# A hybrid mLSTM and sparse-attention block: head operands one head ahead, product buffers dealt anew, branch products with the mLSTM half first

## The chip, the cores and the metric

The kernel runs on one core of a Trainium2 chip. The metric is the device time of one execution in microseconds (us). A profile of one execution, with a row for each instruction and each transfer, shows where that time lies. Engines are called as in the profile: PE (TensorE's matmuls), DVE (VectorE), ACT (ScalarE), POOL (GpSimd), SP (SyncE, which only issues transfers here).

## The reference

T = 1024 tokens, D = 1024. One RMS norm, one wide projection, two mixers, gates, an output projection, and a feed-forward net:

```python
u = rms_norm(h, g_norm_mix); proj = u @ w_in + b_in
mq, mk, mv, mo, mi, mf, nq, nkv, ngate, merge = split_columns(proj, IN_SIZES)
y_m = mlstm_mixer(mq, mk, mv, mo, mi, mf, ...)       # 4 heads x 128, chunks of 128
y_n = nsa_mixer(nq, nkv, ngate, pe_cmp, w_cmp1, w_cmp2, rel_bias)   # 8 heads x 64
branch = einsum('btnw,nwd->btnd', stack([y_m, y_n]), w_branch)
h = h + sum(sigmoid(merge) * branch) @ w_out
f = rms_norm(h, g_norm_ffn)
h = h + (silu(f @ w_gate) * (f @ w_up)) @ w_down; out = rms_norm(h, g_final)
```

The mLSTM head multiplies, for each chunk, a masked decay matrix M (an exponential of it) with q·k, adds the carried state C scaled by S = exp(log_inter − m), and multiplies C by a decay for the next chunk.

## The kernel before, in words

All matmuls are float32 made of three fp32r products (`mm3`, L284: high·high, low·high and high·low parts), so each operand is split once: the high part on ACT, the low part on DVE or Pool.

**Order of the work.** Two ways. The first stages are planned by `Plan` (L63 on): steps are added with hand-written costs, and `run` (L128) deals them to the engines' in-order queues by earliest start and rank; a step with two alternatives goes to the engine that starts it first; a step with `fill=True` is taken only when PE has nothing else. The later stages are written in program order, which is then each engine's queue order.

**First tiles.** For the eight token tiles in the order `XO`, `norm` (L500) makes the norm, `trans` (L513) the transposes into UTH/UTL (u, high and low), `p0` (L544) the NSA values and gate columns, `forms` (L598) the sums of u that the products need. Merge tile 0 (one of 16 tiles of the merge gates' pre-activation, `merge_steps` L659, `merge_half` L679: 24 matmuls a half, its eviction on ACT at L686, then a store) lies between them as fill; both halves are evicted into piece ("x3", 1).

**Products.** The projection's other columns are 12 pairs of 256 columns (`PAIRS` L689). Each is made with seven products in place of eight (`product` L827), from raw weights (`load_raw` L699, pieces dealt by `RAWS` L693), whose sums are split (`prep` L739, operand buffers dealt by `WRING` L694) and whose results are combined (`finish` L769). Within this run `gates` (L903) writes the decay tables M and S to DRAM (d_M, d_S), and `compress` (L998) makes the compressed keys and values: it loads a DRAM copy, adds position columns for 32 windows (L1017, DVE or Pool) and multiplies by w_cmp (L1022).

**mLSTM heads.** `head_load(h)` (L1101) loads v, k, q, M, S, o on SP's queue, S and M by a broadcast read; `core(h)` (L1112) transposes v (L1125), masks M on Pool (L1133; half of head 0's on DVE), copies the decays out of S (L1134), multiplies S by q, then works through 8 chunks (L1143 to L1165), norms and gates, and stores d_ym. Merge tiles 1 to 3 (`merge_B` L1216) are fill beside them. The d_u tiles, parts of u that had been put aside in DRAM, are read back ahead of that by Pool's queue, and VHL (the NSA values, 2 MB) too, wherever the plan finds its place free.

**Attention and merge tiles 4 to 13.** A scheduler of its own; `load_pair` (L1287) loads a pair's q, k and bias tables (QA, KH, KL, FB, FW), for pair 0 on Pool's queue.

**Branch stage.** Merge tiles 14 and 15 run while `load_y` (L1740) reads the y tiles: its step k issues tile k's loads (one of 512 KB for the four mLSTM tiles, two for the four NSA tiles) into a ring of six and splits tile k − 2 into YH and YL (NSA tiles: a sum on DVE first, L1753). A merge tile yields 16 times (`fm_tile` L1248: eight k steps a half, 24 matmuls) and after its fifth k step of the first half it splits the weight of the next job (`split` L243: ACT at L256, then Pool in quarters at L262 or DVE at L264). Then come the branch products d = 0 to 7: for each token half, b = 0 (mLSTM, YH tiles 0 to 3) and b = 1 (NSA, 4 to 7), 12 matmuls each, times the sigmoid of the stored merge gate, added and split.

```python
for z, _ in enumerate(merge_tile(j, gring, psD, 8)):
    if z % 3 == 1:
        next(ly, None)
```

After that the output projection and the feed-forward net, a second plan that the change doesn't touch.

## Time and profile before

| | |
|---|---|
| three runs | 1581.93, 1582.65, 1582.60 us (median 1582.6) |
| profiled execution | 1581.21 us |
| its span in the profile | 1579.4 us (1.8 us lie outside) |
| PE busy in the span | 1543.7 us (98%) |
| DVE, ACT, POOL busy | 1161.1, 772.9, 294.5 us |
| mean granted clock of PE | 0.988 |

A row of the trace names the start, the duration, the engine, the line, the operation, output <- input; in brackets the idle time of the engine before it and what ended it. From 780 us on, the feed-forward net and what leads to it, the stretches show PE busy almost without a break.

### The profile page before, as it was taken

What the parts mean: (1) busy time and instruction counts of PE and PEld (TensorE: products, weight loads), DVE (VectorE), ACT (ScalarE), POOL (GpSimd) and SP (SyncE); (2) the same over time, 40 slices, a digit from 0 to 9 for tenths busy, and PEclk for the clock granted to TensorE, in tenths of its full rate; (3) what the DMA queues carried; (4) which work ended last, traced back from release to release, by engine and by line L of the source; (5) the groups of instructions that cost most, each with busy time, mean ns of one, the idle gap of its engine ahead of it and who ended that gap; (6) DMA issues with size and microseconds to landing.
All of it is one profiled execution on the core that took longest, in us unless ns stands there. A gap on an engine that the chain in (4) does not pass through costs nothing.

```text
span 1579.4 us, 22540 instructions
## 1 busy us (share of the span) xinstructions
PE 1543.7 (98%) x7810; PEld 1304.3 (83%) x7810; DVE 1161.1 (74%) x2390; ACT 772.9 (49%) x1654; POOL 294.5 (19%) x410
## 2 busy tenths in 40 slices
PE   8998999989899999999999999999999999999997
PEld 7887888888699988888788888888888888888886
DVE  5988677657698868884656677666666666988996
ACT  5533333355588868784444453333333333454443
POOL 4658755223111311002002000000000000000130
PEclk9999999999999999999999999999999999999999
DMA  6656674598523632216556324222222223750302
GB/s 180 204 144 199 206 247 134 144 296 164 151 57 103 106 103 71 85 47 219 163 160 227 107 81 133 94 80 80 81 88 86 81 80 115 272 192 22 107 0 107
DMA packets 169899, 205.84 MB, mean 130 GB/s; under 512 B 10265, under 2 KB 128311, under 8 KB 169530
## 3 DMA queue, kind: packets, MB, share of 16 engines
q1 hardware_dynamic: 156584, 179.43, 36.3%
q0 software_dynamic: 12912, 24.65, 6.6%
q8 instruction: 61, 1.00, 0.3%
q14 instruction: 52, 0.43, 0.1%
q10 hardware_dynamic: 290, 0.33, 0.1%
HBM read 149.75 MB, written 62.48 MB: 134 GB/s over the span
## 4 chain that ended last, share of the span: by engine, by line
PE 89%; DVE 4%; DMA 4%; ACT 2%; POOL 1%; issue 1%; SPq 0%; DVEq 0%; ACTq 0%; POOLq 0%
PE PS L286 15%; PE PS L287 15%; PE PS L285 15%; PE PSA L285 5%; PE PSA L287 5%; PE PSA L286 5%; PE T L1437 4%; PE d L285 2%; PE d L287 2%; PE d L286 2%; PE obank L1457 2%; PE obank L1459 2%; PE br L286 2%; PE br L287 2%; PE br L285 2%; DMA XB<-d_S 1%
## 5 line engine op out<-in xcount | busy, mean ns | idle before, releaser
L1840 DVE TENSOR_TENSOR sl<-PS,sl 128x512 f32<-128x512 f32 x182 | 123.5, 688 | 100.8 <-PE PS L287 100.3
L1446 DVE TENSOR_TENSOR TL<-T,TH 128x512 fp32r<-128x512 f32 (+1 forms) x184 | 103.3, 581 | 31.8 <-ACT TH L1442 30.7
L1840 POOL TENSOR_TENSOR acc<-acc 128x512 f32<-128x512 f32 x6 | 9.2, 1545 | 617.6 <-DVE acc L1840 617.5
L1840 DVE TENSOR_TENSOR sl<-sl,sl 128x512 f32<-128x512 f32 (+1 forms) x130 | 88.4, 687 | 21.9 <-DMA d_h<-sl 7.2
L1442 ACT ACTIVATE TH<-T 128x512 fp32r<-128x512 f32 (+1 forms) x184 | 90.3, 510 | 28.7 <-PE T L1437 26.0
L1843 ACT ACTIVATE sl<-sl 128x512 f32<-128x512 f32 (+1 forms) x77 | 48.6, 632 | 57.9 <-PE PS L286 34.4
L1457 PE MATMUL obank<-TH,VHL 128*128 128x256 f32 x264 | 75.4, 309 | 0.0
L285 PE MATMUL d<-UTH,whi 128*128 128x512 f32 x176 | 71.9, 409 | 1.0 <-ACT mg L1274 0.7
L287 PE MATMUL d<-UTH,wlo 128*128 128x512 f32 x176 | 69.1, 392 | 0.0
L286 PE MATMUL d<-UTL,whi 128*128 128x512 f32 x176 | 69.0, 392 | 0.0
L1459 PE MATMUL obank<-TL,VHL 128*128 128x256 f32 x264 | 68.1, 282 | 0.0
L285 PE MATMUL PSA<-UTH,wOwhi 128*128 128x512 f32 x156 | 65.0, 417 | 2.3 <-ACT wOwhi L444 2.2
L285 PE MATMUL PS<-q 128*128 128x512 f32 x172 | 66.9, 389 | 0.0
L286 PE MATMUL PS<-q 128*128 128x512 f32 x172 | 66.9, 389 | 0.0
L287 PE MATMUL PS<-q 128*128 128x512 f32 x172 | 66.9, 389 | 0.0
L287 PE MATMUL PSA<-UTH,wOwlo 128*128 128x512 f32 x164 | 64.9, 396 | 0.0
L1843 ACT ACTIVATE q<-sl 128x512 fp32r<-128x512 f32 x74 | 43.1, 623 | 42.3 <-PE PS L286 32.2
L262 POOL TENSOR_TENSOR wlo<-raw,whi 128x256 fp32r<-128x256 f32 x44 | 32.1, 761 | 169.6 <-ACT whi L256 129.0
L286 PE MATMUL PSA<-UTL,wOwhi 128*128 128x512 f32 x156 | 62.0, 397 | 0.0
L1843 ACT ACTIVATE wh<-sl 128x512 fp32r<-128x512 f32 x39 | 24.6, 631 | 58.2 <-PE PS L286 40.8
L285 PE MATMUL br<-YH,whi 128*128 128x512 f32 x128 | 50.5, 395 | 2.0 <-ACT YH L281 2.0
L286 PE MATMUL br<-YL,whi 128*128 128x512 f32 x128 | 50.7, 396 | 0.5 <-DVE YL L282 0.5
(1380 smaller groups left out, 5075.7 us busy)
## 6 DMA issues: line engine op xcount, KB each, us to landing
d_gu<-sl SPq DMA_DIRECT2D x44, 256.0 KB, 2.2
rA<-in_w_in SPq DMA_DIRECT2D x18, 512.0 KB, 4.7
q<-d_mg SPq DMA_DIRECT2D x32, 256.0 KB, 3.0
d_rep<-d_row POOLq DMA_DIRECT2D x8, 960.0 KB, 6.6
sl<-in_w_down SPq DMA_DIRECT2D x15, 512.0 KB, 3.6
sl<-d_gu SPq DMA_DIRECT2D x15, 512.0 KB, 4.9
ra<-in_w_gate SPq DMA_DIRECT2D x14, 512.0 KB, 3.8
ra<-in_w_up SPq DMA_DIRECT2D x13, 512.0 KB, 4.5
```

The source lines that it names most:

```text
L262: nc.gpsimd.tensor_tensor(lo[:, zs], v[:, zs], cast32(hi)[:, zs], ALU.subtract)
L285: nc.tensor.matmul(ps, ah, bh, start=first, stop=False)
L286: nc.tensor.matmul(ps, ah, bl, start=False, stop=False)
L287: nc.tensor.matmul(ps, al, bh, start=False, stop=last)
L1437: nc.tensor.transpose(pt[:, z, P * r:P * r + P], e, ident)
L1442: nc.scalar.activation(hl[0][:, 0:m], pt[:, 0:m], AF.Copy)
L1446: nc.vector.tensor_tensor(hl[1][:, 0:m], pt[:, 0:m], cast32(hl[0])[:, 0:m], ALU.subtract)
L1457: nc.tensor.matmul(po, vv, th[:, z, :], start=(st[1] == 0), stop=False)
L1459: nc.tensor.matmul(po, vv, tl[:, z, :], start=False, stop=(st[1] == st[2]))
L1840: return pl.step(alts, lambda e: ENG[e].tensor_tensor(out_(), x(), y(), alu), reads, writes, **kw)
L1843: return pl.step((("ACT", cost),), lambda e: nc.scalar.activation(out_(), x(), fn), reads, writes, **kw)
```

## The change

It has five parts. *First tiles*: the norms are made in pairs, one tile ahead, with a small Newton step of five DVE operations for two tiles; p0 adds its bias in one DVE operation, and Pool copies the gate columns out; merge tile 0's halves become ordinary steps of a raised rank, with a piece each (x3 and g21). *Products*: raw pieces and operand buffers are dealt out anew (the first six operands in turn from two buffers); the last pair makes q = 4 third and holds its finish until q = 7. *Compression*: the windows' costs change. *mLSTM heads*: the decays are read by one broadcast load from d_S (DEC); M, q, k, v, S, o get new places, S that of v after v's transposes (head 0 has one of its own); masks and S·q are made on Pool one head ahead; the key weighting may go to ACT; the d_u tiles are restored in the last pair; VHL is loaded ahead of the last head, into the places that head 2 had for k, v and o. *Branch stage*: `load_y` steps at z % 2; the products of d = 0 and 1 run all b = 0 first, then b = 1, with eight gate pieces. The tail of the branch loop for d ≥ 2, `values` (the transposes of v, moved out of `core`) and some lines of tile sizes are left out here.

```diff
@@ -37,6 +37,7 @@
+MA_ = (60, 60)
@@ -497,18 +498,33 @@
-        def norm(i):
-            x_, st = xb[i], stA[:, i, :]
-            s = sb_[i] = K(st)
-            stp("ACT", 1250.0, lambda: nc.scalar.activation(sqA, flat(x_.ap), AF.Square, accum_out=st[:, 0:1]), [x_], [s, sq_A])
-            stp("DVE", 160.0, lambda: nc.vector.tensor_scalar(st[:, 0:1], st[:, 0:1], 1.0 / D, EPS, ALU.mult, ALU.add), (), [s])
-            stp("ACT", 210.0, lambda: nc.scalar.activation(st[:, 1:2], st[:, 0:1], AF.Sqrt), tabs[-1:], [s])
-            stp("DVE", 800.0, lambda: rstd_b(st), (), [s])
...
+        def norm(*ii):
+            n = XO.index(ii[0])
+            st = stA[:, n:n + len(ii), :]
+            s = K(st)
+            hbs = []
+            for i in ii:
+                sb_[i] = s
+                stp("ACT", 1250.0, lambda i=i: nc.scalar.activation(sqA, flat(xb[i].ap), AF.Square, accum_out=stA[:, XO.index(i), 0:1]), [xb[i]], [s, sq_A])
+            stp("DVE", 160.0, lambda: nc.vector.tensor_scalar(st[:, :, 0:1], st[:, :, 0:1], 1.0 / D, EPS, ALU.mult, ALU.add), (), [s])
+            stp("ACT", 210.0, lambda: nc.scalar.activation(st[:, :, 1:2], st[:, :, 0:1], AF.Sqrt), tabs[-1:], [s])
...
+            def newton():
+                y, v, t = (st[:, :, n:n + 1] for n in (2, 0, 3))
+                nc.vector.reciprocal(y, st[:, :, 1:2])
+                nc.vector.tensor_tensor(t, y, y, ALU.mult)
+                nc.vector.tensor_tensor(t, t, v, ALU.mult)
+                nc.vector.tensor_scalar(t, t, -0.5, 1.5, ALU.mult, ALU.add)
+                nc.vector.tensor_tensor(y, y, t, ALU.mult)
+            stp("DVE", 950.0, newton, (), [s])
+            for i in ii:
...
+            return hbs
@@ -561,13 +577,12 @@
-            stp("DVE", 420.0, lambda: nc.vector.tensor_tensor(vt, n4(ps.ap[:, 0:256]), n4(BB[:, 0:256]), ALU.add), [ps] + b_BB, [vb])
-            stp("DVE", 180.0, lambda: nc.vector.tensor_tensor(GT[:, i, :], ps.ap[:, 256:288], BB[:, 256:288], ALU.add), [ps] + b_BB, [b_GT])
+            stp("DVE", 450.0, lambda: nc.vector.tensor_tensor(VT[:, i % 2], ps.ap[:, 0:288], BB, ALU.add), [ps] + b_BB, [vb])
+            stp("Pool", 300.0, lambda: nc.gpsimd.tensor_copy(GT[:, i, :], VT[:, i % 2, 256:288]), [vb], [b_GT])
@@ -638,7 +653,7 @@
@@ -650,10 +665,23 @@
+        HN = {}
...
+        def tile(i):
+            n = XO.index(i)
+            trans(i, HN[i])
+            if n + 3 < NT:
+                load_x(XO[n + 3])
+            if n % 2 == 0:
+                norms(n + 1)
+            p0(i)
...
+        def norms(n):
+            HN.update(zip(XO[n:n + 2], norm(*XO[n:n + 2])))
+        load_x(XO[3])
+        norms(1)
...
-            load_x(XO[XO.index(i) + 2])
-            trans(i, norm(i))
-            p0(i)
+            tile(i)
@@ -676,12 +704,12 @@
-        def merge_half(t, half, mt, o, reads):
+        def merge_half(t, half, mt, o, reads, fill=True):
...
-                    [hb, lb] + reads(n), [ps], fill=True)
+                    [hb, lb] + reads(n), [ps], fill=fill)
@@ -690,17 +718,17 @@
-        RAWS = ["r1 r2", "g20 g10", "r0 r1", "r2 g20", "g10 r0", "r1 r2", "g20 g10", "r0 r1", "r2 g20", "g10 r0", "r2 g20", "r1 r0"]
-        WRING = ("w1", "w3", "w0", "w2")
+        RAWS = ["r1 r2", "r0 g20", "g10 r1", "r2 r0", "g20 g10", "r1 r2", "r0 g20", "g10 r1", "r2 r0", "g20 g10", "r1 r2", "r0 g20"]
+        WRING = ("w0", "w2", "w1", "w3")
...
-        def load_raw(m, after=0.0):
+        def load_raw(m, khs=(0, 1)):
...
-            for kh in range(2):
+            for kh in khs:
@@ -737,7 +765,7 @@
-            nm = WRING[nop[0] % 4]
+            nm = WRING[(nop[0] - 6) % 4 if nop[0] > 5 else 2 + nop[0] % 2]
@@ -851,11 +879,14 @@
+                if (m, 4) in pb:
+                    finish(m, (1, 0), pb[m, 4], v[3])
...
-                finish(m, (1, 0), ps, v[3])
+                if 3 in v:
+                    finish(m, (1, 0), ps, v[3])
@@ -877,26 +908,25 @@
-            if n < 2:
-                load_x(XO[n + 6])
-            trans(i, norm(i))
-            p0(i)
+            tile(i)
...
-            merge_half(0, z, mA, ("x3", 1), lambda n, z=z: [x for i in range(4 * z, 4 * z + 4) for x in (ub[i][0::2] if n >= 4 else ub[i][1::2])])
+                load_raw(1, (0,))
+            pA.boost = -MA_[z]
+            merge_half(0, z, mA, ("x3 g21".split()[z], 1), lambda n, z=z: [x for i in range(4 * z, 4 * z + 4) for x in (ub[i][0::2] if n >= 4 else ub[i][1::2])], fill=False)
...
-        load_raw(1)
+        load_raw(1, (1,))
...
-        seq += [(NP - 1, q) for q in (1, 2, 6, 7, 4, 5, 3)]
-        for n in range(4):
+        seq += [(NP - 1, q) for q in (1, 2, 4, 6, 7, 5, 3)]
+        for n in range(2):
@@ -970,6 +1000,8 @@
+            sd = d_S[:, P - 1:P]
+            load("Pool", 16, [(DEC, bass.AP(tensor=sd.tensor, offset=sd.offset, ap=[[0, P], [P, 32]]))], [b_MS], [b_dec], cost=700.0)
@@ -1015,7 +1047,7 @@
-                pA.step((("DVE", 1150.0), ("Pool", 1700.0)), windows, [kb, b_c], [fb_])
+                pA.step((("DVE", 1700.0), ("Pool", 4000.0)), windows, [kb, b_c], [fb_])
@@ -1037,16 +1069,68 @@
+        ubr = []
...
+        def restore():
+            ubr.extend([x for i in range(NT) for n, x in enumerate(ub[i]) if not (i % 2 and n % 2 == 0)])
+            for j in range(4):
+                cs = slice(P * (2 * j + 1), P * (2 * j + 2))
+                b = K(True, prior=fsb[4, j])
+                load("Pool", 512, [((UTH, UTL)[z][:, 0:4, cs], d_u[j][z]) for z in range(2)], [dub[j]], [b], cost=1400.0)
+                ubr.append(b)
...
+        HB = {}
+        HS = [("v2", "v3", "g10", "v0", "g20", "v1"), ("b0", "b1", "b2", "b3", "b4", None), ("g21", "v2", "v3", "g11", "v1", None), ("r1", "g01", "g10", "r0", "g20", None)]
...
+        def head_load(h, keys):
+            for key in keys:
+                n = "qkvMoS".index(key)
+                b = HB[h, n] = slot(HS[h][n]) if HS[h][n] else HB[h, 2]
+                if key in "MS":
+                    r0 = (d_M if key == "M" else d_S)[h:h + 1, :]
+                    src = bass.AP(tensor=r0.tensor, offset=r0.offset, ap=[[0, P], [4 * P, NT], [1, P]])
+                    load("SP", 512, [(lambda b=b: v8c(b), src)], [b_MS], [b], cost=600.0)
+                else:
+                    load("SP", 512, [(lambda b=b: flat(b.ap), d_mx[key][h])], [dst[key, h]], [b], cost=600.0)
...
+        v8c = lambda b: b.ap.rearrange("p a (c t) -> p (a c) t", t=P)
...
+        def values(h):
...
+        def scale_q(h):
+            SB, q = HB[h, 5], HB[h, 0]
+            for z in range(4):
+                zs = slice(2 * z, 2 * z + 2)
+                stp("Pool", 900.0, lambda zs=zs: nc.gpsimd.tensor_tensor(v8c(SB)[:, zs], v8c(q)[:, zs], v8c(SB)[:, zs], ALU.mult), [q], [SB])
...
+        def mask(h):
+            MB = HB[h, 3]
+            for z in range(4):
+                zs = slice(2 * z, 2 * z + 2)
+                stp("Pool", 900.0, lambda zs=zs: nc.gpsimd.tensor_tensor(v8c(MB)[:, zs], causal[:, None, :].to_broadcast([P, 2, P]), v8c(MB)[:, zs], ALU.subtract), b_rows[8:9], [MB])
...
-        b_MS, b_gc = K(True), K(True)
+        b_MS, b_gc, b_dec = K(True), K(True), K(True, prior=small + [sb_[i] for i in range(NT)])
+        DEC = MSC[:, 876:908]
...
-            if n > 3:
+            if n > 1:
@@ -1057,23 +1141,20 @@
+            if (m, q) == (NP - 1, 4):
+                restore()
...
+            if (m, q) == (8, 3):
+                head_load(0, "MqkS")
+                mask(0)
+                scale_q(0)
...
@@ -1092,48 +1173,15 @@
-        ring("dec", [MSC[:, 578 + 8 * z:586 + 8 * z] for z in range(2)], small)
...
-            stp("Pool", 250.0, lambda: nc.gpsimd.memset(MV[:, :, MD:MD + 1], 1.0), (), [MVb])
-            dec, ss = take("dec"), take("ss")
-            for z in range(2):
-                pv = K()
...
-            for z in range(4):
-                zs = slice(2 * z, 2 * z + 2)
-                if h == 0 and z < 2:
-                    stp("DVE", 400.0, lambda zs=zs: nc.vector.tensor_tensor(v8(MB)[:, zs], causal[:, None, :].to_broadcast([P, 2, P]), v8(MB)[:, zs], ALU.subtract), b_rows[8:9], [MB])
-                else:
-                    stp("Pool", 900.0, lambda zs=zs: nc.gpsimd.tensor_tensor(v8(MB)[:, zs], causal[:, None, :].to_broadcast([P, 2, P]), v8(MB)[:, zs], ALU.subtract), b_rows[8:9], [MB])
-            stp("DVE", 150.0, lambda: nc.vector.tensor_copy(dec.ap, v8(SB)[:, :, 127]), [SB], [dec])
-            for z in range(2):
-                ew(ANY, lambda z=z: SB.ap[:, z, :], lambda z=z: q.ap[:, z, :], lambda z=z: SB.ap[:, z, :], ALU.mult, [q, dec], [SB])
+            ss = take("ss")
@@ -1146,7 +1194,13 @@
-                stp("DVE", 340.0, lambda: nc.vector.tensor_scalar(KW[c].ap, pa_.ap[:, 128:256], E_.ap[:, 127:128], None, ALU.mult), [pa_, E_], [KW[c]])
...
+                def kw(e):
+                    if e == "DVE":
+                        nc.vector.tensor_scalar(KW[c].ap, pa_.ap[:, 128:256], E_.ap[:, 127:128], None, ALU.mult)
+                    else:
+                        nc.scalar.activation(KW[c].ap, pa_.ap[:, 128:256], AF.Copy, scale=E_.ap[:, 127:128])
+                pA.step((("DVE", 340.0), ("ACT", 340.0)), kw, [pa_, E_], [KW[c]])
@@ -1161,7 +1215,7 @@
-                        stt(350.0, lambda: CN.ap, lambda: CN.ap, dec.ap[:, c:c + 1], lambda: o(pu), ALU.mult, ALU.add, [pu, dec], [CN])
+                        stt(350.0, lambda: CN.ap, lambda: CN.ap, DEC[:, 4 * c + h:4 * c + h + 1], lambda: o(pu), ALU.mult, ALU.add, [pu, b_dec], [CN])
@@ -1216,22 +1270,35 @@
-                merge_half(t, z, mB, (("g00", "g01")[t % 2], z), lambda n: ubr if n == 4 else [])
...
+                merge_half(t, z, mB, ("g00", z), lambda n: ubr if n == 4 else [])
...
+        head_load(0, "vo")
+        values(0)
+        head_load(1, "Mqkv")
+        mask(1)
...
-        head_load(0)
-        head_load(1)
+        values(1)
+        head_load(1, "So")
+        scale_q(1)
+        merge_B(2, ("r2", "w0", "w2"))
...
-        head_load(2)
+        head_load(2, "Mqkv")
+        mask(2)
+        values(2)
+        head_load(2, "So")
+        scale_q(2)
+        merge_B(3, ("r2", "w1", "w3"))
...
-        head_load(3)
-        for t_ in range(2, NMB):
-            merge_B(t_, ("r2", ("w0", "w1")[t_ % 2], ("w2", "w3")[t_ % 2]))
+        head_load(3, "Mqkv")
+        mask(3)
+        values(3)
+        head_load(3, "So")
+        scale_q(3)
...
-        core(3)
...
+        core(3)
@@ -1759,7 +1826,7 @@
-                if z % 3 == 1:
+                if z % 2 == 1:
@@ -1771,19 +1838,57 @@
-        load_gates(0, 0)
-        for d in range(8):
+        wide = Pieces([q1_tile(n, F32)[:, z, :] for n in (5, 3) for z in range(4)])
+        gring, narrow = wide, gring
+        W = {}
...
+        def branch(d, half, b):
+            hs = slice(512 * half, 512 * half + 512)
+            sg = sgs[d, half]
+            nc.scalar.activation(sg[b], sg[b], AF.Sigmoid)
+            wh, wl = W[d]
+            ps = psD.tile([P, 512], F32, name=f"br{d}{half}{b}", tag="D", bufs=8)
+            for k in range(4):
+                kk = 4 * b + k
+                mm3(ps, wh[:, kk, :], wl[:, kk, :], YH[:, kk, hs], YL[:, kk, hs], k == 0, k == 3)
+            return ps, sg, hs
...
+        def gate(d, half, b, ps, sg, hs, join=True):
+            nc.vector.tensor_tensor(sg[b], ps, sg[b], ALU.mult)
+            if b == 1 and join:
+                blend(d, half)
...
+        def blend(d, half):
+            sg, hs = sgs.pop((d, half)), slice(512 * half, 512 * half + 512)
+            nc.vector.tensor_tensor(sg[0], sg[0], sg[1], ALU.add)
+            split_evict(UTH[:, d, hs], UTL[:, d, hs], sg[0])
...
+        FIRST = [(d, half, b) for b in range(2) for d in range(2) for half in range(2)]
+        for d, half, b in FIRST[:4]:
+            load_gates(d, half)
+        for n, (d, half, b) in enumerate(FIRST):
+            if b == 0 and half == 0:
+                W[d] = ws.get(j_br[d])
+            x = branch(d, half, b)
+            if n == 0:
+                ws.split(j_br[1])
+                ws.dma(j_br[2])
+            if n == 6:
+                ws.split(j_br[2])
+                ws.dma(j_br[3])
+            gate(d, half, b, *x)
+            if n == 5:
+                gring = narrow
+                gring.n = 0
+                load_gates(2, 0)
+        for d in range(2, 8):
...
```

More of the change, by code (lines that the diff above doesn't have):

```diff
@@ L640, in body @@
         idle(2)
-        trans(0, norm(0))
+        trans(0, norm(0)[0])
         split_p0()
@@ L710, in load_raw @@
                     parts = [(lambda b=b: rows4(b), wk[:, ks, c:c + 256])]
-                load("SP", 512, parts, (), [b], cost=900.0, after=after)
+                load("SP", 512, parts, (), [b], cost=900.0)
         def sums(m, n):
@@ new lines, in body, with go @@
+        v8c = lambda b: b.ap.rearrange("p a (c t) -> p (a c) t", t=P)
+        def values(h):
+            MVb = HB[h, "MV"] = slot(f"x{2 * (h % 2)}")
+            MV = XR[:, 2 * (h % 2)].rearrange("p (c t) -> p c t", t=MD + 1)
+            stp("Pool", 250.0, lambda: nc.gpsimd.memset(MV[:, :, MD:MD + 1], 1.0), (), [MVb])
+            for z in range(2):
+                pv = K()
+                def go(pv=pv, z=z):
+                    for c in range(4):
+                        nc.tensor.transpose(pv.ap[:, P * c:P * c + P], v8c(HB[h, 2])[:, 4 * z + c, :], ident)
+                stp("PE", 440.0, go, [HB[h, 2], b_id], [pv])
+                stp("ACT", 560.0, lambda pv=pv, z=z: nc.scalar.activation(MV[:, 4 * z:4 * z + 4, 0:MD], four(pv.ap), AF.Copy), [pv], [MVb])
@@ L1064, in body @@
                 compress(1)
+            if (m, q) == (8, 3):
+                head_load(0, "MqkS")
+                mask(0)
+                scale_q(0)
         table(EXPLN)
-        ubr = [x for i in range(NT) for n, x in enumerate(ub[i]) if not (i % 2 and n % 2 == 0)]
-        for j in range(4):
-            cs = slice(P * (2 * j + 1), P * (2 * j + 2))
-            b = K(True, prior=fsb[4, j])
-            load("Pool", 512, [((UTH, UTL)[z][:, 0:4, cs], d_u[j][z]) for z in range(2)], [dub[j]], [b], cost=1400.0)
-            ubr.append(b)
-        HB = {}
         SC = {}
@@ L1782, in body @@
                     load_gates(d + 1, 0)
-                hs = slice(512 * half, 512 * half + 512)
-                sg = sgs.pop((d, half))
-                for b in range(2):
-                    nc.scalar.activation(sg[b], sg[b], AF.Sigmoid)
                 if d == 7 and half == 0:
@@ L1793, in body @@
                 for b in range(2):
-                    ps = psD.tile([P, 512], F32, name=f"br{d}{half}{b}", tag="D", bufs=8)
-                    for k in range(4):
-                        kk = 4 * b + k
-                        mm3(ps, wh[:, kk, :], wl[:, kk, :], YH[:, kk, hs], YL[:, kk, hs], k == 0, k == 3)
-                    nc.vector.tensor_tensor(sg[b], ps, sg[b], ALU.mult)
-                if d < 7 and half == 0:
-                    ws.dma(n + 2)
-                    ws.split(n + 1)
-                if d == 5 and half == 1 or d == 6 and half == 0:
-                    ws.dma(n + 3)
-                if d == 6 and half == 1:
-                    ws.split(n + 2, True)
-                    ws.dma(n + 4)
-                nc.vector.tensor_tensor(sg[0], sg[0], sg[1], ALU.add)
-                split_evict(UTH[:, d, hs], UTL[:, d, hs], sg[0])
+                    x = branch(d, half, b)
+                    gate(d, half, b, *x, False)
+                    if b == 0:
+                        continue
+                    if d < 7 and half == 0:
+                        ws.dma(n + 2)
+                        ws.split(n + 1)
+                    if d == 5 and half == 1 or d == 6 and half == 0:
+                        ws.dma(n + 3)
+                    if d == 6 and half == 1:
+                        ws.split(n + 2, True)
+                        ws.dma(n + 4)
+                    blend(d, half)
     if "MX" in dbg:
```

43 lines of the change are left out of this document (13 added, 30 removed).

## The prediction

> **What bounds the kernel now.** I read the page first, then the busy time in stretches of 20 us, then TensorE's waits, and last the rows around each wait.
>
> ```profile
> span 1579.4 us, 22540 instructions
> PE 1543.7 (98%) x7810; PEld 1304.3 (83%) x7810; DVE 1161.1 (74%) x2390; ACT 772.9 (49%) x1654; POOL 294.5 (19%) x410
> ```
>
> TensorE is the bound: it stands idle for 1579.4 − 1543.7 = 35.7 us of the whole span. No edit takes a matmul away or adds one, so the change can win only idle time and the time run at a reduced clock behind it. The stretches say where these are (columns: stretch, length, then busy time and instructions of PE, weight loads, DVE, ACT, POOL, then granted clock, DMA share, GB/s).
>
> ```profile
> 40.00:60.00 20.00, 19.63 (x131) 18.14 (x130) 19.58 (x44) 13.80 (x27) 13.79 (x20) 1.00 0.53 159
> 60.00:80.00 20.00, 17.80 (x74) 14.02 (x74) 17.29 (x26) 10.26 (x18) 11.88 (x13) 0.91 0.69 243
> 140.00:160.00 20.00, 15.73 (x77) 13.18 (x76) 18.12 (x16) 6.67 (x11) 19.24 (x22) 0.91 0.81 241
> 160.00:180.00 20.00, 20.00 (x86) 16.37 (x85) 11.06 (x19) 5.39 (x9) 9.73 (x13) 0.92 0.83 261
> 320.00:340.00 20.00, 16.80 (x106) 14.87 (x104) 8.79 (x27) 10.87 (x39) 5.65 (x9) 0.91 1.14 304
> 340.00:360.00 20.00, 18.54 (x120) 16.98 (x121) 15.61 (x55) 10.78 (x42) 5.40 (x9) 0.91 0.89 289
> 400.00:420.00 20.00, 14.84 (x66) 11.02 (x65) 9.38 (x39) 8.68 (x30) 3.48 (x10) 0.83 0.57 190
> 740.00:760.00 20.00, 17.50 (x69) 13.32 (x68) 12.34 (x15) 9.07 (x14) 3.81 (x4) 0.93 0.69 255
> 760.00:780.00 20.00, 20.00 (x88) 16.49 (x87) 13.67 (x19) 10.98 (x17) 0.00 (x0) 0.98 0.56 175
> ```
>
> I price a place as idle time plus (1 − clock) × length. The first tiles (60 to 80): 2.2 + 1.8 = 4.0 us. The compression (140 to 180): 4.27 + 1.8 + 1.6 = 7.7. The mLSTM heads (320 to 360): 3.2 + 1.46 + 3.6 = 8.3. The start of attention (400 to 420): 5.16 + 3.4 = 8.6. The branch products (740 to 780): 2.5 + 1.4 + 0.4 = 4.3. Together 32.9 us: the most that this change can gain at the places that it touches. Behind 780 us nothing of it runs. TensorE's waits name the releasers:
>
> ```profile
> PE PSA L1022 <- DMA VW<-in_w_cmp: 4.3, 1, 4.3
> PE PSA L1155 <- DVE Rg L1148: 2.7, 1, 2.7
> PE S0s L1355 <- DVE nx L1382: 2.4, 1, 2.4
> PE PSA L285 <- ACT wOwhi L444: 2.2, 1, 2.2
> PE br L285 <- ACT YH L281: 2.0, 2, 1.7
> PE PSA L1160 <- ACT XR L1165: 1.8, 1, 1.8
> ```
>
> Time behind a hole is lost at a lower clock: the 4.27 us hole before 160 is followed by 0.91 and 0.92, which is 3.4 us; the 2.2 us one by 0.91, 1.8 us. [...]
>
> **First tiles.** The 2.2 us wait is for an operand split on ACT, and ACT was held by merge tile 0's second eviction, which waits for the store of its first half out of the same piece:
>
> ```profile
> 67.41 5.49 DMA d_mg<-XR
> 73.00 0.69 ACT L686 ACTIVATE XR<-PSA,COLS 128x512 f32<-128x512 f32 x1 [1.66 <-DMA d_mg<-XR]
> 77.64 2.20 POOL L440 TENSOR_TENSOR X<-RG,X 128x256 fp32r<-128x256 f32 x2 [0.75 <-ACT X L444]
> ```
>
> The two halves get two pieces (x3, g21), so that wait goes, and 4.0 us at most with it. The norms in pairs save about half of the one-column DVE operations, and eight short adds go over to Pool as copies: that helps while DVE is full (19.58 of 20 us at 40 to 60). Against it: the next product but one needs the last form, on Pool at 77.64 to 79.84, hardly later than the hole at 74.26; and the first operands share two buffers instead of four, so that a late split shows at once. The merge halves, no longer fill, can also push a product back. I take −2, with −4 to +2.
>
> **Compression.** The windows (L1017) ran on Pool by a cost of 1700 that they did not hold:
>
> ```profile
> 152.94 8.06 POOL L1017 TENSOR_SCALAR VW<-VW,COLS 128x126 f32<-128x126 f32 x8
> 170.38 1.25 DVE L1017 TENSOR_SCALAR VW<-VW,COLS 128x126 f32<-128x126 f32 x4 [1.28 <-DMA VW<-d_kc]
> 149.67 7.77 DMA VW<-in_w_cmp
> ```
>
> Four take about 4.0 us on Pool and 1.25 on DVE. With the new costs (DVE 1700, Pool 4000) they go to DVE. But the wait is also for a weight transfer issued at 149.67 and landed at 157.44, about the moment at which the fourth of the eight windows ends; faster windows alone leave that transfer, which starts when its buffer is free. DVE was busy 18.12 us of that stretch and gets about 2.5 us more. I take half of 7.7: −4, with −7 to 0.
>
> The new deal of raw pieces and operand buffers and the last pair's order (q = 4 third, its finish held until q = 7) move no work; they stand beside TensorE at 20.00 of 20 us (160 to 180): 0 while operands lie ready, and 4.0, the price of the hole at 74, for each that does not.
>
> **mLSTM heads and the start of attention.** Head 1's mask is made late because S and M are loaded late, in a DMA share of 1.14:
>
> ```profile
> 335.95 2.82 POOL L1133 TENSOR_TENSOR XB<-cst,XB 128x256 f32<-128x256 f32 x4 [7.22 <-DMA XB<-d_M]
> 321.24 16.14 DMA XB<-d_S
> 337.40 0.69 DVE L1134 COPY MSC<-XB 128x8 f32<-128x8 f32 x1 [2.82 <-DMA XB<-d_S]
> ```
>
> S takes 16.14 us to land; the decay copy (L1134) holds the DVE queue for 2.82 us, and L1148, for which TensorE waits 2.7, stands behind it. The change loads the decays once through DRAM, drops that copy, loads head 0's M, q, k and S some products early and every later head's one head ahead, lets ACT take the key weighting from DVE, and gives the S·q product to Pool: with the masks 8 operations of 2.82 / 4 = 0.7 us a head there, 5.6 us. Restoring the d_u tiles (eight loads on Pool's queue) is issued in the last pair and leaves this crowd. So both the 2.7 and the 1.8 wait (ACT behind a merge tile's late raw weights) can go; new order constraints (S goes into v's buffer only after v's transposes; merge tiles 2 and 3 now ahead of their heads) may leave some. At the start of attention:
>
> ```profile
> 409.23 1.06 ACT L256 ACTIVATE whi<-rawS 128x1024 fp32r<-128x1024 f32 x1 [10.71 <-DMA rawS<-in_w_in]
> 406.33 0.29 DVE L1382 CUSTOM_DVE_ANT_0 E0w<-S0w,FB 128x128 f32<-128x128 f32 x1 [3.16 <-DMA FB<-d_rep]
> 208.56 0.58 POOL L411 DMA_DIRECT2D VHL<-d_vh  x1 [1.15 <-PE PSA L1022]
> VHL<-d_vh POOLq DMA_DIRECT2D x1, 2048.0 KB, 12.1
> FB<-d_rep POOLq DMA_DIRECT2D x2, 512.0 KB, 9.8
> RG<-in_w_in POOLq DMA_DIRECT2D x1, 32.0 KB, 6.5
> ```
>
> The raw weights of the next merge tile go into slot r0, which is now head 3's mask and not its output gate, so they come some us earlier and ACT is held less. FB comes no earlier by itself: pair 0's loads start when the heads' buffers come free. And VHL, 2 MB and 12.1 us, issued at 208.56 before, must now wait for head 2, whose k, v and o lie in its place; it stands on Pool's queue ahead of FB. For heads and start together the bounds are 16.9 us of gain (8.3 + 8.6) and 7 us of loss (VHL's 12.1 less the 5 us of idle time that it would overlap). I take −6, a third of the gain, since FB's landing and not the heads sets the start of attention.
>
> The new broadcast load of the decays reads 4096 single words on Pool's queue. The nearest row is a load of 1024 short rows, 6.5 us (RG, 32 KB); four times that is 26 us, while the first use is over 100 us later and nothing but the d_rep copies stands behind it: 0, at most +2.
>
> **Branch products.** Here I expect a loss.
>
> ```profile
> 740.98 1.05 ACT L256 ACTIVATE whi<-raw 128x1024 fp32r<-128x1024 f32 x1
> 742.10 3.81 POOL L262 TENSOR_TENSOR wlo<-raw,whi 128x256 fp32r<-128x256 f32 x4 [10.34 <-DMA d_mg<-q]
> 743.00 1.61 DVE L1753 TENSOR_TENSOR q<-q 128x1024 f32<-128x1024 f32 x1 [1.13 <-DMA q<-d_yn]
> 754.54 1.22 DVE L1753 TENSOR_TENSOR q<-q 128x1024 f32<-128x1024 f32 x1
> 755.79 1.15 ACT L281 ACTIVATE YH<-q 128x512 fp32r<-128x512 f32 x2 [1.97 <-DVE q L1753]
> 748.73 0.39 PE L285 MATMUL br<-YH,whi 128*128 128x512 f32 x1
> ```
>
> The generator that loads and splits the y tiles takes one step at z % 3 == 1 of a merge tile's sixteen: five steps in tile 14, five in tile 15. Tile 15 splits the first branch weight after its fifth k step, one generator step into the tile, that is right behind y3: 740.98 on ACT, 742.10 on Pool. With z % 2 == 1 tile 14 takes eight steps and tile 15 its two before the split: all of y4 to y7 then stand ahead of it in ACT's queue. These are NSA tiles whose sums are paced by loads and DVE. From 743.00 the DVE chain takes about 3.15 us a tile (754.54 − 743.00 is 11.5 for three, with a load wait in it): y7's sum at 752.4, its two YH halves done 2.4 us later, the weight's high part 1.05, the first Pool quarter some 0.9: the first branch matmul near 756, where it was 748.73 and TensorE runs dry. That the mLSTM half goes first helps nothing then: its y tiles were split long before, and the weight is what is late. What was 4.3 becomes 7.3 of hole and 3.4 of clock (the price behind the 4.27 us hole) = 10.7: **+6**. If the loads, issued earlier, bring the chain 2 us forward: 5.3 + 1.8 − 4.3 = +3. If y7 comes no earlier than now (755.79 + 1.15 + 1.05 = 758): 9.3 + 3.4 − 4.3 = +8. The second half's waits for YH (2.0) go and are counted in the 4.3; the second weight is needed two products, 5.4 us, after the first and is split right behind it.
>
> **Sum.** −2 − 4 − 6 + 6 = −6 on the profiled 1581.21 (span 1579.4 and 1.8 around it): 1575.2. The median, 1582.6, lies 1.4 above that run: 1576.6 us.
>
> **The rivals.** (1) *All covers hold.* First tiles −3.6, compression −6, heads and start −7, and the branch hole at its lower bound, +3: −13.6, 1569. For it: each wait has its own cause that the edits take away. Against: FB and the w_cmp transfer are DMA, and the hole follows from the program order. (2) *Pool holds DVE.* The masks and S·q are now 8 Pool operations a head beside the DVE chain. At 147.64 one DVE operation took 5.86 us beside Pool work where others of its form take 0.7:
>
> ```profile
> 147.64 5.86 DVE L447 SCALAR_TENSOR_TENSOR Rg<-Rg 128x512 fp32r<-128x512 f32 x1
> 153.42 0.68 DVE L447 SCALAR_TENSOR_TENSOR RG<-RG 128x512 fp32r<-128x512 f32 x1
> ```
>
> If half of the six groups of four (2.82 us) of heads 1 to 3 each hold a DVE step on the path, that is 8.5 us, the heads' −6 becomes +2.5, and the sum is +2.5, 1585.1. [...] (3) *Slower: VHL in front of pair 0's loads.* FB lands at 406.3, so its transfer starts near 406.3 − 9.8 = 396.5; VHL's 12.1 us fit in front of it only if it is issued by 384. From then on each us of delay costs one, up to the 7 us above, and the heads' gain ends in that wait: −2 − 4 + 7 + 6 = +7, 1589.6. For it: VHL now needs head 2 to be done. Against it: one head still follows on TensorE, and 2 MB can land beside that. That the change does nothing at all is excluded by its operations on the path.
>
> **How the numbers follow.** About 0.2%, 3.2 us, is what a measurement of this kernel can tell from no change. Forecast 0.48, (1) 0.16, (2) 0.18, (3) 0.18. The forecast's own range, from its terms' bounds, is 1571 to 1582; the other cases take it from 1566 to 1588. Faster: 0.16 and most of 0.48; same: its upper end and half of (2); slower: (3) and a little of (2): 0.60, 0.21, 0.19.
>
> **What would show it.** Right: no wait at 74 us on L444; L1017 on DVE and the compression's wait shorter but there; no wait for L1148 near 341; no VHL issue at 208 but one behind head 2; and a hole of 5 to 9 us before the first branch matmul, released by ACT's or Pool's split of the weight. Wrong: if the branch products start without a hole, the time falls to case (1) or under it; if FB lands after 412, (3).

## The result, and the profile after

| | before | changed |
|---|---|---|
| median | 1582.56 us (1581.93 to 1582.65, 4 runs) | 1595.48 us (1592.66 to 1597.51, 4 runs) |
| ratio | | 1.0081, 95% interval 1.0064 to 1.0099 |
| profiled execution, span | 1581.21, 1579.4 us | 1597.51, 1595.7 us |
| mean granted clock | 0.988 | 0.985 |

The change made the kernel slower by 0.8%; the forecast was 1576.6 us with a range up to 1588. The profiled run of the changed kernel is the slowest of its four, and that of the kernel before lies 1.4 us below its median, so its span is 16.3 us longer where the medians differ by 12.9.

PE does the same 7810 instructions in both. So the start of the last matmul of a group is a mark that both traces have, and the lines of one source line give it. First the kernel before, then the changed one (columns: line, engine, operation, tiles, count; shortest, median and longest ns; start of the first and of the last):

```profile
L285 PE MATMUL d<-UTH,whi x176: 387/393/505, 435.2 to 748.1; 128*128 128x512 f32 x176
L285 PE MATMUL PSA<-UTH,wOwhi x156: 387/389/778, 48.2 to 396.9; 128*128 128x512 f32 x156
L285 PE MATMUL br<-YH,whi x128: 389/389/632, 748.7 to 840.3; 128*128 128x512 f32 x128
L285 PE MATMUL PSA<-UTH,wOwlo x100: 387/389/774, 55.0 to 316.9; 128*128 128x512 f32 x100
```

```profile
L286 PE MATMUL d<-UTH,whi x176: 387/393/505, 444.9 to 757.7; 128*128 128x512 f32 x176
L286 PE MATMUL PSA<-UTH,wOwhi x156: 388/389/486, 50.2 to 398.3; 128*128 128x512 f32 x156
L286 PE MATMUL br<-YH,whi x128: 389/389/792, 766.7 to 855.6; 128*128 128x512 f32 x128
L286 PE MATMUL PSA<-UTH,wOwlo x100: 387/389/632, 71.1 to 320.3; 128*128 128x512 f32 x100
```

The products (the last wOwlo) end 3.4 us later, the heads and their merge tiles (the last wOwhi) 1.4 later, merge tile 15 (the last d) 9.6 later, the branch products 15.3 later, the span 16.3. So the heads give 2.0 back, attention from its start on loses 8.2, the branch stage 5.7, and the untouched rest 1.0. Two places, the start of attention and the branch stage, make most of the result. PE's waits name them:

```profile
PE S0w L1422 <- POOL KH L1352: 11.9, 1, 11.9
PE br L286 <- ACT whi L257: 8.2, 1, 8.2
PE PSA L1107 <- DMA XB<-d_mv: 3.3, 1, 3.3
PE PSA L288 <- DVE wOwhi L438: 2.8, 1, 2.8
PE PSA L539 <- DVE XR L448: 2.7, 2, 1.9
PE PSA L1054 <- DMA VW<-in_w_cmp: 2.2, 2, 1.8
```

The waits of before for L1148, L1165 and the split at 74 are gone, the one for w_cmp fell from 4.3 to 2.2. In their place stand a wait for head 0's v (L1107), for the normed tile of the first stage (L539) and for another operand at 77 (L288). The stretches that changed most, in the windows view of the changed kernel (columns: stretch, its length, busy time of PE, PEld, DVE, ACT and Pool, PE's granted clock, DMA share, GB/s):

```profile
40.00:60.00 20.00, 17.29 (x107) 15.53 (x106) 19.69 (x35) 9.98 (x19) 14.75 (x23) 0.91 0.37 105
220.00:240.00 20.00, 18.19 (x76) 13.76 (x75) 13.26 (x13) 7.78 (x11) 13.87 (x15) 1.00 0.65 222
400.00:420.00 20.00, 6.70 (x22) 4.22 (x20) 0.88 (x9) 1.76 (x6) 9.06 (x21) 0.67 1.32 274
760.00:780.00 20.00, 13.26 (x48) 10.66 (x49) 7.41 (x10) 9.68 (x14) 2.80 (x4) 0.74 0.63 201
```

**The start of attention.** From the timeline of the changed kernel, first SP's queue:

```profile
383.95 0.32 SPq L412 DMA_DIRECT2D d_ym<-VW  x1
```

Pool's instructions from there on (in brackets the idle time ahead of an instruction, and what ended it):

```profile
389.81 0.58 POOL L412 DMA_DIRECT2D VHL<-d_vh  x1 [22.04 <-ACT XR L1219]
390.39 2.10 POOL L1360 DMA_DIRECT2D QA<-d_q  x4
392.47 1.38 POOL L1370 DMA_DIRECT2D KH<-d_kh  x2
393.84 0.68 POOL L1370 DMA_DIRECT2D KL<-d_kl  x1
399.47 0.68 POOL L1370 DMA_DIRECT2D KL<-d_kl  x1 [4.95 <-DMA VHL<-d_vh]
...
413.07 0.62 POOL L1352 CAST KH<-CMP 128x512 fp32r<-128x512 f32 x1
```

And PE's first matmul of attention:

```profile
413.74 0.53 PE L1422 MATMUL S0w<-KH,QA 128*128 128x192 f32 x1 [11.92 <-POOL KH L1352]
```

VHL is issued at 389.81, 5.9 us behind the issue of the store of head 2's result out of VW, whose place it takes. That store lands after 5.2 us (the last column), at 389.15:

```profile
d_ym<-VW SPq DMA_DIRECT2D x1, 512.0 KB, 5.2
```

VHL's row names another releaser, an ACT eviction (L1219); head 3's last one ahead of the issue ended at 389.62. So it is inferred from the times, and not shown, that the store is what held VHL. Pair 0's loads stand behind it on Pool's queue and begin at 390.39 (384.81 before). Eight transfers are issued one behind the other; the ninth, a KL load, is issued at 399.47, when VHL has landed (after 9.4 us). KH's last columns are written on Pool behind the last of these loads, and PE waits for them until 413.74.

**The branch stage.** The timeline of the changed kernel around the first branch product, DVE:

```profile
763.34 1.22 DVE L1820 TENSOR_TENSOR q<-q 128x1024 f32<-128x1024 f32 x1 [0.96 <-DMA q<-d_yn]
```

ACT:

```profile
764.60 1.15 ACT L282 ACTIVATE YH<-q 128x512 fp32r<-128x512 f32 x2 [3.02 <-DVE q L1820]
765.65 1.04 ACT L257 ACTIVATE whi<-raw 128x1024 fp32r<-128x1024 f32 x1
```

PE:

```profile
758.12 0.39 PE L288 MATMUL d<-UTH,wlo 128*128 128x512 f32 x1
766.75 0.79 PE L286 MATMUL br<-YH,whi 128*128 128x512 f32 x1 [8.24 <-ACT whi L257]
767.34 0.63 PE L287 MATMUL br<-YL,whi 128*128 128x512 f32 x1
767.76 0.63 PE L288 MATMUL br<-YH,wlo 128*128 128x512 f32 x1
...
771.97 0.39 PE L286 MATMUL br<-YH,whi 128*128 128x512 f32 x1
772.20 0.40 PE L287 MATMUL br<-YL,whi 128*128 128x512 f32 x1
```

This is the hole that was forecast: the weight's high part follows y7's two YH halves on ACT at once, and PE stands idle for 8.24 us. Behind it the clock costs more: the twelve matmuls from 766.75 on take 5.2 us until the next starts at 771.97, mostly 0.43 us apart, where they later start 0.23 us apart (granted clock 0.51 from 766.75 to 772.00, 1.00 from there to 780). That is 2.5 us lost. The prediction's price, (1 − clock) × length, would put 5.2 us on this stretch (0.74 over 20 us): 2.5 us is what twelve slow matmuls lose, so the rest of the low clock lies in the hole itself (0.69 from 758.50 to 766.75) and is counted twice.

### The profile page after: what moved, and what is told of

The parts are those of the page before. It is cut to its first block, busy times and chain, and to the rows that moved or that the text cites. A ratio compares the mean times of both kernels' runs of the same rounds, so it can differ in the third digit from the quotient of the medians.

```text
span 1595.7 us, 22548 instructions
## 1 busy us (share of the span) xinstructions
PE 1545.5 (97%) x7810; PEld 1304.5 (82%) x7810; DVE 1149.9 (72%) x2334; ACT 779.6 (49%) x1677; POOL 304.9 (19%) x435
## 4 chain that ended last, share of the span: by engine, by line
PE 83%; DMA 7%; DVE 4%; ACT 2%; issue 2%; POOL 1%; SPq 1%; DVEq 0%; POOLq 0%; ACTq 0%
PE PS L287 14%; PE PS L288 14%; PE PS L286 14%; PE T L1504 4%; PE PSA L286 4%; PE PSA L288 4%; PE PSA L287 4%; PE d L286 2%; PE d L288 2%; PE d L287 2%; PE obank L1524 2%; PE obank L1526 2%; PE br L286 2%; PE br L287 2%; PE br L288 2%
## 5 line engine op out<-in xcount | busy, mean ns | idle before, releaser
L1942 DVE TENSOR_TENSOR sl<-sl,sl 128x512 f32<-128x512 f32 (+1 forms) x130 | 88.6, 688 | 22.9 <-DMA d_h<-sl 7.2
L288 PE MATMUL d<-UTH,wlo 128*128 128x512 f32 x176 | 69.1, 393 | 0.0
L288 PE MATMUL PS<-q 128*128 128x512 f32 x172 | 66.9, 389 | 0.0
L288 PE MATMUL PSA<-UTH,wOwlo 128*128 128x512 f32 x164 | 64.8, 395 | 1.3 <-POOL wOwlo L441 1.3
L1526 PEld LDWEIGHTS obank<-TL,VHL 128*128 128x128 f32 x264 | 50.0, 189 | 1.1 <-DVE TL L1513 0.3
```

The source lines that it names most:

```text
L288: nc.tensor.matmul(ps, al, bh, start=False, stop=last)
L1526: nc.tensor.matmul(po, vv, tl[:, z, :], start=False, stop=(st[1] == st[2]))
L1942: return pl.step(alts, lambda e: ENG[e].tensor_tensor(out_(), x(), y(), alu), reads, writes, **kw)
```

## The experiments

The last three columns are times between marks, from each kernel's profiled run: up to the last wOwhi, from there to the last d, from there to the last br. They say in which stage a time was lost, but not to the last us: equal programs reached the first mark between 390.4 and 397.8 us (e1 and e3, which differ only in the branch stage), while the second and third times of equal stages agree within 1.6 us. The ratios are to runs of the kernel before from the same round, whose medians lie between 1582.0 and 1583.9.

| kernel | median, us | ratio to before, 95% | to heads' end | attention | branch |
|---|---|---|---|---|---|
| before | 1582.6 | | 396.9 | 351.2 | 92.2 |
| changed | 1595.5 | 1.0064 to 1.0099 | 398.3 | 359.4 | 97.9 |
| e1 VHL last | 1584.1 | 0.9993 to 1.0019 | 390.4 | 350.1 | 98.3 |
| e2 y at z % 3 | 1594.5 | 1.0056 to 1.0096 | 395.2 | 358.4 | 99.5 |
| e3 both | 1587.0 | 1.0003 to 1.0026 | 397.8 | 349.4 | 100.2 |
| e4 before, branch order alone | 1587.5 | 1.0016 to 1.0035 | 394.7 | 352.3 | 99.1 |
| e5 second weight early | 1576.4 | 0.9939 to 0.9974 | 397.4 | 350.6 | 88.9 |
| e6 before, branch with it | 1576.6 | 0.9949 to 0.9975 | 395.0 | 352.0 | 88.6 |
| e7 single norms | 1576.9 | 0.9945 to 0.9973 | 396.4 | 349.2 | 88.7 |
| e8 head 0 late | 1571.8 | 0.9914 to 0.9943 | 391.1 | 350.3 | 88.5 |
| e9 VHL later still | 1563.2 | 0.9845 to 0.9906 | 391.0 | 341.6 | 87.4 |
| e10 merge halves as fill | 1586.1 | 1.0007 to 1.0032 | 404.8 | 350.8 | 88.2 |
| e11 windows on DVE | 1572.5 | 0.9896 to 0.9951 | 394.5 | 350.0 | 88.3 |

**e1, VHL behind pair 0's loads.** The edit, on the changed kernel:

```diff
-        load("Pool", 2048, [(lambda: vb_.ap.rearrange("p i n c -> p (i n c)"), d_vh)], [b_dvh], [vb_], cost=700.0)
...
     load_pair(0)
+    nc.gpsimd.dma_start(VHL.rearrange("p i n c -> p (i n c)"), d_vh)
     behind(0)
```

> The changed kernel, but VHL (2 MB) is issued on Pool's queue behind pair 0's loads instead of ahead of them; nothing else moves. Theory (order on Pool's queue): VHL waits for head 2's store, and pair 0's loads, whose own places are free some 15 us earlier, only wait because they stand behind it. Then the 11.9 us hole at the start of attention goes, the loss between 400 and 440 falls from 19.9 to 8 or less, and the median from 1595.5 to 1584 or less. Rival (amount of data): the same 6.9 MB must land before attention can run, so the hole shrinks by 3 us at most or comes back as a wait for VHL at the first output products: 1592 or more. Rival (heads): head 3 itself ends late: no change.

The median fell by 11.4 us to that of before, attention by 9.3. The 11.9 us wait is gone; Pool's timeline in e1 has:

```profile
366.31 2.15 POOL L1357 DMA_DIRECT2D QA<-d_q  x4 [7.12 <-ACT Rg L1202]
```

Pair 0's loads begin at 366.31, 24 us earlier than in the changed kernel (16 us, measured from the end of the heads, which this profiled run reached 7.9 us sooner): their places had been free, and only the order on the queue held them. That is the theory of the queue's order. The rival of the amount of data was not wholly wrong: a wait of 6.3 us is left at S1w, of which e9 tells.

**e2, the y tiles at z % 3, and e3, both.**

```diff
-                if z % 2 == 1:
+                if z % 3 == 1:
                     next(ly, None)
```

> The changed kernel, but the generator of the y tiles steps at z % 3 == 1 again; the mLSTM half still comes first. Theory (the weight's split stands behind y7 in ACT's queue): the weight is split right behind y3, the 8.2 us hole ahead of the first branch product goes whole and no wait for YH takes its place, since four mLSTM products (11 us) cover the last NSA tiles: 1595.5 - 9.5 = 1586. Rival (the y tiles' loads are late in any case): a hole of 4 us or more stays, at the first NSA product: 1591 or more.

> Both edits on the changed kernel: VHL behind pair 0's loads, and the generator's step at z % 3 == 1. If both theories hold the gains add: 1595.5 - 12 - 9.5 = 1574, faster than the kernel before by 8. If either hole only moves, 1580 or more.

The theory fell: the branch stage did not get shorter (99.5 and 100.2, after 97.9). The wait of PE is still there, 9.5 us in e2 and 10.7 in e3, and the profile still names a weight split. **e4** shows where it is, the new order of products on the kernel before (diff as in the change, from `wide = Pieces` on):

> The kernel before with one part of the change alone: the branch products of d = 0 and 1 with all mLSTM halves first and eight gate pieces, the generator still at z % 3 == 1. Theory: the order in itself is a gain, it takes away the waits for YH (2.0 us and the low clock behind them, 4.3 to 5 us in all): 1582.6 - 4.5 = 1578. Rival: the waits only move to the gates or to the second weight: 1582 or more.

It is 0.25% slower than before, where a gain was expected. The timeline of e4, PE:

```profile
752.91 0.39 PE L287 MATMUL br<-YH,wlo 128*128 128x512 f32 x1
762.54 0.80 PE L285 MATMUL br<-YH,whi 128*128 128x512 f32 x1 [9.24 <-ACT whi L256]
```

And ACT:

```profile
756.01 1.15 ACT L281 ACTIVATE YH<-q 128x512 fp32r<-128x512 f32 x2 [1.98 <-DVE q L1753]
...
760.91 0.63 ACT L1781 ACTIVATE q<-q 128x512 f32<-128x512 f32 x1 [1.88 <-DMA q<-d_mg]
761.45 1.04 ACT L256 ACTIVATE whi<-raw 128x1024 fp32r<-128x1024 f32 x1
```

The first weight is early (its products run up to 752.91), but after two mLSTM products the order turns to d = 1 and needs the second weight. That one is split behind the first product's sigmoid in ACT's queue, and so behind y7 and a load of gates (760.91): 761.45. The old order needs the second weight only after four products of d = 0. With z % 2 it is the first weight that is late (8.24 us), with z % 3 the second (9.24 us here), and each costs about the same.

**e5 and e6, the second weight early.** On e3 (e5) and on e4 (e6):

```diff
-                if z % 3 == 1:
+                if z % 3 == 1 and (j < 15 or z < 10):
                     next(ly, None)
+        ws.split(j_br[1], True)
         for _ in ly:
             pass
```

> The changed kernel with VHL behind pair 0's loads, the generator at z % 3 == 1, and its last two steps (y6 and y7) held back until the second branch weight has been split, that split on ACT and Pool right behind merge tile 15. Theory (second weight): in the run with z % 3 alone the 9.5 us hole was not ahead of the first product but ahead of the third, which needs the second weight, whose split stood behind y7 in ACT's queue; now both weights are split ahead of y6 and y7, the hole goes whole, the loss between 740 and 780 falls from 13.3 to 2 or less, and the median lands near 1574. Rival (the NSA tiles are late in any case): the hole moves to the first NSA product, 11 us behind the first mLSTM product: 5 us or more stay, 1580 or more.

> The kernel before with the mLSTM half first, eight gate pieces and both weights split ahead of y6 and y7; nothing else of the change. Theory (second weight): the order of the branch products is a gain once its weights are early: the loss of 5.5 us between 740 and 780 goes, 1583 - 5 = 1578. Rival (NSA tiles late in any case): 1582 or more.

Both came as the second-weight theory had it: the branch stage takes 88.9 and 88.6 us, 3.3 and 3.6 less than before and 9.0 and 9.3 less than in the changed kernel, and of the hole PE keeps two waits in e5, 0.34 and 0.52 us, behind 771. So the new order of products with both weights early is a gain, 5.4 us in the median of e6 against the kernel before in its round and 3.6 in the stage, and the place of two weight splits turns it into a loss. No run has the weights early with the old order, so what the order is worth by itself stays open.

**e7, single norms.** On e5, `norms(n + 1)` after every tile, one tile at a time.

> As the run with the second weight early, but the norms of the first tiles are made one tile at a time, still one tile ahead. Theory (a pair of norms puts four DVE operations of 0.7 us at once in front of the next tile's transposes): the waits of 1.9 and 0.9 us for the normed tile near 43 and the low clock behind them go, the loss between 40 and 60 falls from 5.6 to 3 or less, some 3 us faster than that run. Rival (the new load order of the x tiles or the DVE work as a whole is the cause): no change within 1 us.

No difference in the median (1576.9 against 1576.4). The first products begin 2 us earlier, but a wait of 6.9 us for the gates' row (L954) appears ahead of 81, and the products end at 320.0 (320.3). The term "pairs" is not what makes the first tiles late, or not alone; this stays open.

**e8, head 0 late.** On e5, `after=290000` for head 0's mask and S·q.

```diff
-... [q], [SB])
+... [q], [SB], after=0.0 if h else 290000.0)
...
-... b_rows[8:9], [MB])
+... b_rows[8:9], [MB], after=0.0 if h else 290000.0)
```

> As the run with the second weight early, but the mask and the S times q product of head 0 may not be planned before 290 us. Theory (head 0's eight Pool operations and their wait for the transfers stand in front of operand splits on Pool's queue near 214 to 231): the three waits near 232 to 237 and the low clock behind them go, the loss between 220 and 240 falls from 3.0 to 0.5, some 2.5 us faster than that run, if nothing is then late at 320. Rival (buffers dealt anew cause it): the loss at 220 to 240 stays.

Faster by 4.6 us in the median, where 2.5 were expected; the two intervals touch, so the size is not sharp. In the changed kernel Pool's timeline had this:

```profile
225.37 4.13 POOL L1115 TENSOR_TENSOR VW<-VW 128x256 f32<-128x256 f32 x3 [5.49 <-DMA VW<-d_mq]
...
231.16 2.41 POOL L441 TENSOR_TENSOR wOwhi<-Rg,wOwhi 128x256 fp32r<-128x256 f32 x2
```

And PE's these waits:

```profile
231.93 0.50 PE L288 MATMUL PSA<-X,wOwhi 128*128 128x512 f32 x1 [0.41 <-POOL wOwhi L441]
235.66 0.50 PE L286 MATMUL PSA<-X,wOwlo 128*128 128x512 f32 x1 [0.85 <-ACT wOwlo L445]
236.93 0.50 PE L288 MATMUL PSA<-X,wOwlo 128*128 128x512 f32 x1 [0.53 <-DVE wOwlo L438]
```

Head 0's S·q, needed some 100 us later, waits 5.49 us at the head of Pool's queue for q to land, and an operand split that PE needs at once stands behind it. In e8's windows view that stretch of PE is full (1.8 us idle in the changed kernel, 2.65 in e5):

```profile
220.00:240.00 20.00, 20.00 (x90) 16.57 (x89) 14.07 (x14) 8.27 (x11) 13.68 (x12) 1.00 0.68 235
```

So the hole goes; the other 2 us of the gain are not explained. The products end 5.0 us earlier than in e5 (315.3), but this mark doesn't show the edit: the changed kernel, e1, e2, e3 and e5, equal up to there, end them at 315.1 to 321.5. Early work alone doesn't make the hole either: e7 makes head 0's S·q as early, Pool waits only 1.75 us ahead of it, and PE is full between 220 and 240. The hole comes from where the planner put the wait.

**e9, VHL later still.** On e8, VHL in two pieces behind the first weight split of attention's merge tiles:

```diff
-    nc.gpsimd.dma_start(VHL.rearrange("p i n c -> p (i n c)"), d_vh)
...
+                for n, y in enumerate(merge_tile(j, cp, psC, 1)):
+                    if j == NMB + NMX and n == 5:
+                        for c in (slice(0, 1024), slice(1024, 4096)):
+                            nc.gpsimd.dma_start(VHL.rearrange("p i n c -> p (i n c)")[:, c], d_vh[:, c])
+                    yield y
```

> As the run with head 0 late, but VHL is issued some 5 us later still, in two pieces (512 and 1536 KB) behind the first weight split that merge tile 5 has on Pool. In the runs with VHL behind pair 0's loads a wait of 6.3 us is left at the start of attention: DVE's first write of E0s, for which the profile names no releaser, comes 0.2 us after the landing of the last merge store (issued 392.65, 10.0 us). Theory (VHL's 2 MB slow the store out of a place that E0s takes over): with VHL later the store lands in some 3 us, DVE writes E0s near 396, the 6.3 us wait goes, loss between 380 and 420 from 11.1 to 5 or less, 5 us faster than that run, unless the first output products then wait for VHL (2 us). Rival (DVE waits for something else, such as the bias tables): the wait stays at 6 us.

8.6 us faster than e8, attention 341.6 us where all others have 349 or more. VHL's issue, first in e8, then in e9:

```profile
391.70 0.53 POOL L1383 DMA_DIRECT2D VHL<-d_vh  x1
```

```profile
396.42 1.09 POOL L1394 DMA_DIRECT2D VHL<-d_vh  x2
```

In e8 the last merge store (issued 392.65; the last column is the time to its landing, in us):

```profile
d_mg<-RG SPq DMA_DIRECT2D x1, 256.0 KB, 10.0
```

The first E0s on DVE in e8's timeline:

```profile
402.83 0.29 DVE L1447 CUSTOM_DVE_ANT_0 E0s<-S0s,FB 128x128 f32<-128x128 f32 x1 [7.29 <-issue]
```

And in e9 the same store, and the same E0s:

```profile
d_mg<-RG SPq DMA_DIRECT2D x1, 256.0 KB, 3.6
```

```profile
396.41 0.29 DVE L1450 CUSTOM_DVE_ANT_0 E0s<-S0s,FB 128x128 f32<-128x128 f32 x1 [0.88 <-ACT E0w L1454]
```

392.65 + 10.0 = 402.65, and DVE goes on at 402.83; with the store landed after 3.6 us it goes on at 396.41, when its data are there. "issue" in a row says only that the profile knows no releaser. That E0s takes over the store's place is inferred from these times; that VHL's issue makes the wait, by its time or its two pieces, is shown. The store on SP's queue took 10.0 us with VHL's 2 MB issued on Pool's queue 0.95 us ahead of it, and 3.6 us where VHL was issued at 396.42; how the two share the way, no run here shows.

**e10, merge halves as fill; e11, windows on DVE alone**, each on e8:

```diff
-            merge_half(0, z, mA, ..., fill=False)
+            merge_half(0, z, mA, ..., fill=True)
```

```diff
-                pA.step((("DVE", 1700.0), ("Pool", 4000.0)), windows, [kb, b_c], [fb_])
+                pA.step((("DVE", 1700.0),), windows, [kb, b_c], [fb_])
```

> As the run with head 0 late, but merge tile 0's halves are fill again; they keep their own two pieces. Theory (ordinary steps of raised rank push the DVE and PE work of the first products back): the 3.0 us wait near 77 goes and the loss between 40 and 100 falls from 10.9 to 8 or less. Rival (the two operand buffers and the norms' DVE work are the cause): the loss stays within 1 us, or grows.

> As the run with head 0 late, but all of the compression's windows go to DVE. In the changed kernel the planner still gave more than half of them to Pool, at 1.1 to 1.25 us each, in spite of the cost of 4000. Theory (windows on Pool also hold the operand splits behind them): the loss of 4.9 between 140 and 160 falls to 2.5 or less, 2 us faster. Rival (the w_cmp transfer lands last): a wait of 1.8 us for it stays and the time is within 1 us.

Neither theory held. e10 is 14.2 us slower: the 3.0 us wait near 77 goes, but PE's idle time between 40 and 100 grows from 5.8 to 9.1 us, as its rival allowed; and the planner deals the rest of the run out otherwise, so that PE waits 10.3 us for a w_cmp transfer. So in this plan the halves are better as ordinary steps than as fill. e11 has no difference in the median: PE's idle time between 140 and 160 falls from 3.6 to 0.65 us, as the theory had it, but 4.05 us appear between 220 and 240, for operand splits, most of it for ACT. Both runs show that one edit to the plan moves waits elsewhere; what the edited step alone is worth they don't tell.

## Why the prediction was wrong

It was wrong in sign: −6 became +13, +16.3 between the profiled runs. Two of its steps failed there, heads and start of attention by 12.2 us and first tiles with compression by 9.4; the branch step held. By its steps:

- *Branch products, +6*: right in mechanism and sum. 7.3 us of hole and 3.4 of clock were put, 8.24 and 2.5 measured, so two small misses cancel; +5.7 in the stage. One sentence in it was wrong: that the second weight "is split right behind" the first. It doesn't show while the first is late, but e2, e3 and e4 show that it is the next limit, 9.2 to 10.7 us.
- *Heads and the start of attention, −6*: this is the step that failed most. The heads gave −2.0; the start of attention and what follows gave +8.2: +6.2 together. The rival with VHL in front of pair 0's loads is what happened, and its price of up to 7 us fits; e1 shows it. Its condition was an issue later than 384; it was 389.81, and I gave it 0.18. What I got wrong is when VHL could be issued: "one head still follows" says nothing of the time, and I didn't look for it. The trace of before had it. Head 2's store there was issued at 381.07 and landed 2.7 us later, at 383.8, at the very edge of the condition:

```profile
381.07 0.32 SPq L411 DMA_DIRECT2D d_ym<-XB  x1
```

```profile
d_ym<-XB SPq DMA_DIRECT2D x1, 512.0 KB, 2.7
```

  The path was another one, too. I had FB's landing as what sets the start of attention; in the changed kernel PE's first wait, 11.9 us, is for KH, written on Pool behind the last of the loads, and a second one of 1.3 us follows. A load that was issued at 208.56 before had been given a late condition, in front of the next stage's loads.
- *First tiles −2 and compression −4*: this step failed as well. The products end at +3.4 instead of −6. How much of that the change does is not sharp: the kernel before, e4 and e6, equal up to there, end them at 315.0 to 317.4, the changed kernel and its four equals at 315.1 to 321.5. A gain of 6 us is not in it. The two named waits did go or shrink (74.26; 4.3 to 2.2), but head 0's early work, priced at nothing, put 1.8 us of idle time behind 220 (gone in e8), and the first tiles got new waits at 43 and 77. The cover that I named, operands ready ahead, did not hold. What the norms in pairs alone cost is not settled (e7).
- *Windows by price*: that the windows go to DVE at 1700 and 4000 was wrong: Pool ran 20 of the 32 (24 before). e11, which gives all to DVE, is no faster.
- *Pool holds DVE*: not tried by itself. It would have made heads and start of attention 2.5 us longer by way of the heads; the heads came out 2.0 shorter, so no run here needs it. Its term, DVE steps of the heads held for the 2.82 us of a Pool group, stands in neither kernel's trace: from 318 to 398 us in the changed kernel the longest DVE operation took 1.23 us, and the eight of L1260 took 0.68 to 1.16 us, the longest of them beside head 3's S·q on Pool (364.52 to 367.77). Rows of 3.88 and 4.96 us, like the one of 5.86, stand in the products (150.38 and 197.09); what held them is not shown.
- The decays' broadcast load at nothing: no wait names it in the changed kernel.

The change can be made a gain: e9, with VHL, the last y tiles with the second weight's split, and head 0's early Pool work moved and the rest kept, is the fastest kernel here, 1563.2 us, 0.9875 of the runs of before beside it (0.9845 to 0.9906).

## What to carry to other kernels

When a transfer moves, read what its issue will now wait for, and then every transfer behind it on the same queue; a load with a late condition belongs behind the loads that have none (11.4 us in the median, e1). When products are reordered, list for each the operand that it newly needs first, and put that operand's preparation ahead of work on the same queue that is not needed yet (10.9 us in the medians, from e4 to e6). Work done early is not free: head 0's S·q stood on Pool's queue, with its wait of 5.49 us, in front of an operand split that PE needed at once. Before a rival is given a chance, look in the trace for the row that sets its condition; here it was the landing of head 2's store.
